# A hybrid encoder layer on one core: input projections in pairs by seven products, ahead of a recurrence whose preparation is split in two

## The chip, the cores and the metric

The kernel runs on one core of a Trainium2 chip. The metric is device time in microseconds (us) of one execution. Engines are named as the profile names them: PE (TensorE matmul), PEld (its weight loads), DVE (VectorE), ACT (ScalarE), POOL (GpSimd), SP (SyncE, which issues most DMAs).

## The reference, cut to what matters

Two batches of 512 tokens, width 1024, pass one layer with shared weights.

```python
h = _rmsnorm(x, norm_mix_g[l])
gates, p_a, pq, pkv, pkr = _split(h @ w_in[l], IN_SPLITS)      # 4416 columns
p_a = _token_shift(p_a, shift_mu[l])                           # previous and next token mixed in
y_a = _rwkv7_branch(p_a, ...) @ w_oa[l]
y_b = _mla_branch(pq, pkv, pkr, ...) @ w_ob[l]
g_a, g_b = jnp.split(jax.nn.sigmoid(gates), 2, axis=-1)
x = x + (g_a * y_a + g_b * y_b) @ w_out[l]
h = _rmsnorm(x, norm_ffn_g[l])
gt, up = jnp.split(h @ w_gu[l], 2, axis=-1)
x = x + (jax.nn.silu(gt) * up) @ w_down[l]
```

Branch A is a recurrence over the tokens, forwards and backwards, for 8 heads of 64; each step does

```python
sa = jnp.einsum('bhvk,bhk->bhv', state, kk_t)
state = (state * w_t[:, :, None, :] - sa[..., None] * (kk_t * a_t)[:, :, None, :]
         + v_t[..., None] * k_t[:, :, None, :])
return state, jnp.einsum('bhvk,bhk->bhv', state, r_t)
```

Here r, k and v are projections (`rkv`), w and a come from low-rank products (`w2`), kk is k scaled and normalised in each head, and the output is normalised per head, gets a bonus term and a low-rank gate (`g2`). Branch B is latent attention, 8 heads: queries, keys and values are products of small normalised latents; softmax over 512 keys.

## The kernel before, in words

**Precision.** Most products take operands split into a high and a low part (`split`: a copy on ACT, a subtraction on DVE). `mm3` issues three matmuls for each pair of operands, of 128 rows by 512 columns as a rule. Products of the recurrence, the transposes, and probabilities times values take plain 32-bit operands.

**Front.** Eight tiles of x are normalised and transposed (`norm_T`) into operands `h_hi`, `h_lo` of each batch. `proj` multiplies one tile of 128 columns of w_in with both batches, 8 inner blocks, 48 matmuls. There are 35 tiles: 4 low-rank inputs (w, a, g, x), 12 of r, k, v (`rkv_tiles`, three for each of four head pairs), 16 gates (`gate_tile`), 3 latents. First come the four low-rank tiles, then the low-rank up products (`lora_phase`), the first pair's r, k, v, and the latents. Results go to DRAM tensors (`rwkv_in`, `gate_d`, `mla_d`).

**Recurrence.** A unit is one batch and one pair of heads; there are eight, two batches for each pair in turn. Tokens are cut in 8 chunks of 64, both directions at once. `prep` loads r, k, v, makes the key norm and the bonus term, scans the decays, builds the scaled tiles `kra`, `krb`, `bt`, `kt`, multiplies them to `gx` and `gy`, and transposes (`tb`, `tk`, `vp`). `lanes` solves the triangular systems of all chunks on POOL (31 steps of a multiplication and an addition, tiles `lt`, `el`). `merge` joins the 32-wide halves (`zp`, `xp`). `state` walks the 8 chunks (`s`, `o`, copies `rs`, `sva`, `svb`), and `post` normalises the output.

**Order.** During the recurrence the order of PE is written out by `drive`. It keeps a planned clock, adds a planned cost for every matmul, and always lets the first thread in its list go on whose waiting time is over: state, post, merge, preparation, fill, combine. A thread yields planned microseconds (times 1.2 for state, 1.4 for the others), or a condition. The fill thread has the remaining r, k, v tiles, all gates and the attention; a step of it is one matmul. A unit's preparation goes in one thread, one unit after the other, and its second half waits for the state of two units before. The merge of a unit is planned 40 us after its solve is issued. Outside `drive` the framework orders the instructions.

**Attention** computes keys, values and queries as it needs them, then for each head and 128 queries: scores (`sc`), maximum, exponential, division by the sum, four transposes (`pt`), and for two heads together probabilities times values (`pav`).

**After it.** `combine` multiplies both branches' outputs with w_oa and w_ob (`pab`), scales by the gates and adds; `project` multiplies with w_out (`pwo`). Batch 0 combines and projects, then batch 1. Then come the norms and the feed-forward part, which already takes pairs of blocks by seven products: `gate_up` (`pgA`, `pgB`, `pgC`) and the down products (`dx`, `dy`, `dz`).

Of the kernel before, what the change touches and what calls it, by code (L numbers as in the profile page):

```python
# [47 lines left out]
PB = (5, 1)  # L48
# [22 lines left out]
OFFS = 200000, 150000, 120000, 100000, 0, 0  # L71
# [8 lines left out]
C0 = 18  # L80
PL = 3.5
# [13 lines left out]
ES = 'gg'  # L95
EF = 'gggg'
# [8 lines left out]
def trunk(ctx, tc, outs, x, w_in, w2, g2, w_uq, w_ukk, w_ukv, w_oab, w_out, w_gu, w_down,  # L105
# [42 lines left out]
    nc.sync.dma_start(idn, ident)  # L148
# [16 lines left out]
    rwkv_in = [[dram.tile([P, 8, S], F32, name=f"rwkv_in{b}{p}") for p in range(NPAIR)] for b in range(NB)]  # L165
# [58 lines left out]
    front = ctx.enter_context(ExitStack())  # L224
    psf = ppool(front, "psf")

    def pf(name):
        return psf.tile([P, S], F32, tag="f", bufs=NF, name=name)

    def mg(name):  # L230
        return psf.tile([P, S], F32, tag="mg", bufs=2, name=name)
# [5 lines left out]
    class _PS:  # L237
        def tile(self, shape, dt, tag=None, name=None):
            return psf.tile([P, S], F32, tag=PSTAG[0], bufs=PSTAG[1], name=name)

    class _PF:
        def tile(self, shape, dt, tag=None, name=None):
            return pf(name)

    e_d = [dram.tile([32, CH, CH], F32, name=f"e_d{i}") for i in range(2)]
    nt_d = [dram.tile([32, CH, CH], F32, name=f"nt_d{i}") for i in range(2)]
    bo_d = [[dram.tile([P, S], F32, name=f"bo_d{b}{p}") for p in range(NPAIR)] for b in range(NB)]
    mla_d = [dram.tile([P, 3, S], F32, name=f"mla_d{b}") for b in range(NB)]
    kr_d = [dram.tile([64, S], F32, name=f"kr_d{b}") for b in range(NB)]

# [4 lines left out]
    hst = ctx.enter_context(ExitStack())  # L255
    hp = pool(hst, "h", side="right")
    h_hi, h_lo = [None] * NB, [None] * NB
    for b in HORD:
        h_hi[b] = hp.tile([P, KD, S], F32R, name=f"h_hi{b}")
        h_lo[b] = hp.tile([P, KD, S], F32R, name=f"h_lo{b}")  # L260
    wp = pool(hst, "w1", side="right")
# [4 lines left out]
    def norm_T(t, xt, sp, newps, gcol, hi, lo, name):  # L266

        ss = sp.tile([P, 1], F32, tag="nss", bufs=4, name=f"nss_{name}{t}")
        ht = sp.tile([P, D], F32, tag="nh", bufs=NHB, name=f"nh_{name}{t}")
        nc.scalar.activation(ht, xt, AF.Square, accum_out=ss)  # L270
        rstd_cols(ss, ss, 1, 1.0 / D, RMS_EPS)
        nc.vector.tensor_scalar_mul(ht, xt, ss)
        ts = slice(t * P, (t + 1) * P)
        for g in range(2):
            ps = newps(f"nt_{name}{t}{g}")
            tr4(ps, lambda i: ht[:, (g * 4 + i) * P:(g * 4 + i + 1) * P])
            gs = slice(g * 4, (g + 1) * 4)
            sc = sp.tile([P, 4, P], F32, tag="nsc", bufs=NSB, name=f"nsc_{name}{t}{g}")
            nc.vector.tensor_mul(sc, ps.rearrange("p (k t) -> p k t", k=4),
                                 cc(gcol + g * 4, 4).unsqueeze(2).to_broadcast([P, 4, P]))  # L280
            nc.scalar.copy(hi[:, gs, ts], sc)
            vg(NLO[t * 2 + g]).tensor_sub(lo[:, gs, ts], sc, hi[:, gs, ts])

    def proj(ti, name):
        res = [pf(f"pj_{name}{b}") for b in range(NB)]
        wt = []
        for q in range(2):
            raw = wp.tile([P, 4 * P], F32, tag="wraw", bufs=2, name=f"wraw_{name}{q}")
            nc.sync.dma_start(raw, w_in[ti][:, q * 512:(q + 1) * 512])
            hi = wp.tile([P, 4 * P], F32R, tag="whi", bufs=2, name=f"whi_{name}{q}")  # L290
            lo = wp.tile([P, 4 * P], F32R, tag="wlo", bufs=2, name=f"wlo_{name}{q}")
            split(hi, lo, raw)
            wt.append((hi, lo))
# [1419 lines left out]
```

## Time and profile before

| | |
|---|---|
| median of 2 runs | 1835.03 us (1832.98 to 1837.08) |
| profiled execution | 1835.74 us, span 1834.0 us |
| PE busy | 1734.3 us, 95% of the span |
| DVE, ACT, POOL busy | 1116.9, 771.0, 642.2 us |
| DMA moved | 208.97 MB, 114 GB/s |
| granted PE clock, mean | 0.978 |

A page of the profile gives busy time of each engine, the chain of work that ended last, and groups of instructions with mean durations. A matmul's recorded duration holds its latency, which overlaps with the next one; what it takes of PE's time is seen in the chain, where a piece ends as the next begins. Plain 32-bit matmuls stand as two records each.

### The profile page before, as it was taken

The numbers are of one execution on the slowest core, as the hardware profiler recorded it, in microseconds if no ns is written. First come the engines' busy times: TensorE is split into PE (matmuls) and PEld (weight loads), VectorE is DVE, ScalarE is ACT, GpSimd is POOL, SyncE is SP. The second block draws the span as 40 slices with busy tenths as digits, with TensorE's granted clock in tenths as the row PEclk, the third lists the DMA queues.
The fourth block names the chain that finished last, engine by engine and source line by source line (L and its number), as shares of the span: only waits on it lengthen the run. The fifth ranks groups of instructions, "written<-read, shape, count | busy, mean of one in ns | idle before, by whom it ended". The sixth has DMA issues, their size and how long they took to land.

```text
span 1834.0 us, 31000 instructions
## 1 busy us (share of the span) xinstructions
PE 1734.3 (95%) x11676; PEld 1365.7 (74%) x11676; DVE 1116.9 (61%) x1957; ACT 771.0 (42%) x1496; POOL 642.2 (35%) x992
## 2 busy tenths in 40 slices
PE   6999999999999998899989999699999999989997
PEld 6887766777677775565657979578888888868886
DVE  6633555635364455877786556865655555588757
ACT  5434343333434334656663233333333333335445
POOL 3012345362635536161112123853434333100006
PEclk8999989999999998999999999899999999999999
DMA  4354433425343334212067551022222222274342
GB/s 163 123 175 163 123 107 82 124 71 136 81 125 106 89 113 119 61 36 55 21 233 249 190 178 35 24 81 93 103 95 84 92 81 92 98 273 134 121 139 92
DMA packets 185333, 208.97 MB, mean 114 GB/s; under 512 B 102816, under 2 KB 114464, under 8 KB 185184
## 3 DMA queue, kind: packets, MB, share of 16 engines
q1 hardware_dynamic: 184320, 205.48, 35.4%
q8 instruction: 92, 1.51, 0.3%
q10 hardware_dynamic: 720, 0.98, 0.2%
q0 software_dynamic: 144, 0.52, 0.1%
q14 instruction: 57, 0.47, 0.1%
HBM read 147.70 MB, written 59.24 MB: 113 GB/s over the span
## 4 chain that ended last, share of the span: by engine, by line
PE 70%; DVE 9%; DMA 8%; POOL 5%; issue 3%; ACT 2%; SPq 1%; DVEq 0%; POOLq 0%; ACTq 0%
PE pgC L125 9%; PE pj_gt L125 8%; PE pgB L125 6%; PE pgA L125 6%; PE pj_rkv L125 5%; PE dx L125 5%; PE dy L125 3%; PE s L125 3%; PE pab L125 2%; PE sc L125 2%; PE pav L125 2%; PE pj_mla L125 2%; DMA wor<-in_w_out 2%; PE o L125 2%; PE gx L125 2%
## 5 line engine op out<-in xcount | busy, mean ns | idle before, releaser
L839 POOL TENSOR_TENSOR lt<-lane,el 128x126 f32<-128x126 f32 (+22 forms) x248 | 93.4, 377 | 38.1 <-DMA lane<-nt_d 19.6
L841 POOL TENSOR_TENSOR el<-el,lt 128x126 f32<-128x126 f32 (+22 forms) x248 | 98.6, 398 | 19.0
L125 PE MATMUL pab<-yo,wab 128*128 128x512 f32 x384 | 94.7, 400 | 5.9 <-ACT yo L132 3.2
L125 PE MATMUL pj_gt<-h_hi,whi_gt 128*128 128x512 f32 x240 | 99.2, 413 | 0.0
L125 PE MATMUL pj_gt<-h_hi,wlo_gt 128*128 128x512 f32 x240 | 98.8, 412 | 0.1
L125 PE MATMUL pj_gt<-h_lo,whi_gt 128*128 128x512 f32 x240 | 98.1, 409 | 0.0
L125 PE MATMUL pwo<-woh,m 128*128 128x256 f32 x512 | 93.8, 283 | 0.1
L125 PEld LDWEIGHTS pab<-yo,wab 128*128 128x128 f32 x384 | 71.9, 191 | 26.0 <-DVE wab L133 4.2
L1203 POOL TENSOR_TENSOR s<-uraw 128x512 f32<-128x512 f32 x22 | 29.3, 1330 | 152.1 <-DMA uraw<-in_w_gu 152.1
L125 PEld LDWEIGHTS pwo<-woh,m 128*128 128x128 f32 x512 | 80.3, 192 | 0.6 <-ACT woh L132 0.3
L125 PE MATMUL pj_rkv<-h_hi,wlo_rkv 128*128 128x512 f32 x192 | 79.7, 418 | 0.0
L125 PE MATMUL pj_rkv<-h_lo,whi_rkv 128*128 128x512 f32 x192 | 79.1, 412 | 0.0
L125 PE MATMUL pj_rkv<-h_hi,whi_rkv 128*128 128x512 f32 x192 | 78.3, 408 | 0.0
L125 PE MATMUL pwo<-wol,m 128*128 128x256 f32 x256 | 72.4, 284 | 0.9 <-DVE wol L133 0.9
L1582 POOL TENSOR_TENSOR x<-x,dp 128x512 f32<-128x512 f32 x4 | 6.3, 1590 | 178.1 <-DVE x L1581 178.1
L1271 DVE TENSOR_TENSOR p<-p,pgC 128x512 f32<-128x512 f32 x22 | 15.1, 687 | 86.9 <-PE pgC L125 86.9
L919 ACT COPY sva<-s 64x128 f32<-64x128 f32 x64 | 16.5, 258 | 104.6 <-PE s L125 96.3
L1050 POOL TENSOR_TENSOR g<-g 128x512 f32<-128x512 f32 x16 | 24.9, 1554 | 92.7 <-DVE g L1048 84.5
L466 POOL TENSOR_SCALAR lut<-lut 128x512 f32<-128x512 f32 x32 | 20.5, 641 | 98.4 <-ACT lut L464 98.1
L125 PEld LDWEIGHTS pj_gt<-h_hi,wlo_gt 128*128 128x128 f32 x240 | 45.1, 188 | 9.5 <-DVE wlo_gt L133 0.8
L125 PEld LDWEIGHTS pj_gt<-h_hi,whi_gt 128*128 128x128 f32 x240 | 45.1, 188 | 8.6
L125 PEld LDWEIGHTS pj_gt<-h_lo,whi_gt 128*128 128x128 f32 x240 | 45.1, 188 | 8.4
(1559 smaller groups left out, 5552.9 us busy)
## 6 DMA issues: line engine op xcount, KB each, us to landing
graw<-in_w_gu SPq DMA_DIRECT2D x22, 512.0 KB, 3.5
uraw<-in_w_gu SPq DMA_DIRECT2D x22, 512.0 KB, 3.5
a_d<-a SPq DMA_DIRECT2D x21, 512.0 KB, 3.3
w<-in_w_down SPq DMA_DIRECT2D x42, 256.0 KB, 4.1
x<-in_x SPq DMA_DIRECT2D x16, 512.0 KB, 8.2
rwkv_in<-lut SPq DMA_DIRECT2D x32, 256.0 KB, 2.0
gate_d<-gtt SPq DMA_DIRECT2D x32, 256.0 KB, 2.5
wab<-in_w_oab SPq DMA_DIRECT2D x32, 256.0 KB, 3.6
```

The costliest lines, as they stand in the source:

```text
L125: pin(nc.tensor.matmul(out, lhsT, rhs, start=start, stop=stop, **kw), n if out.shape[0] > 64 else n / 2)
L466: nc.gpsimd.tensor_scalar(t, t, f, f, op0=ALU.mult, op1=ALU.add)
L839: eng.tensor_mul(lv, lane[:, s, s + 1:].unsqueeze(1).to_broadcast([P, m_, n]), el[:, 0:m_, s].unsqueeze(2).to_broadcast([P, m_, n]))
L841: eng.tensor_add(ev, ev, lv)
L919: nc.scalar.copy(sva[HA, :, c], s2[HA])
L1050: nc.gpsimd.tensor_add(g_[:, 0], g_[:, 0], g_[:, 1])
L1203: vg(ES[min(j, 1)]).tensor_add(s1, a21, a22)
L1271: nc.vector.tensor_add(p1, p1, x_)
L1582: nc.gpsimd.tensor_add(xs(1, t, 1), xs(1, t, 1), p5[t])
```

## The change

**Projections.** All projections come before the recurrence. Two tiles of 128 columns and the two batches form a two-by-two block product with the inner dimension halved; `pair` makes it from seven products of 12 matmuls (in place of eight) with sums of weight blocks on DVE and sums of results. The batch-side operands are `H11`, `H21`, `H22`, `U1` to `U4`, made at the start from the norms of x. The tile that is left over goes through `single`. `early` begins four gate pairs before all operands exist.

**Work beside the projections.** `Fill` puts steps of other work between the products: latent norms, keys and values, queries (multiplied with the rotary tables and the softmax scale), the low-rank up products, and the key norms and bonus terms of all units. Their results go to DRAM (`k_d`, `v_d`, `q_d`, and a ninth plane of `rwkv_in`). The low-rank up product takes 64-row halves of its weights for the two directions, instead of zero-padded 128 rows.

**Recurrence.** Units go batch by batch. `prep_a` loads, scans, makes `gx` and starts the solve; `prep_b` makes `krb`, `gy` and the transposes. They are two threads; `prep_a` may be three units ahead of the state, so `kra`, `arb`, `e_d`, `nt_d` get a third set. The copies `rs`, `z` and those from `xp` go to ACT.

**Fill of the recurrence.** Attention loads its keys, values and queries; the division by the sum comes after the product with the values, by a broadcast that four transposes make. Then come the attention branch's products of both batches, branch A's of batch 0, and the output projection of batch 0, whose result goes to DRAM. Branch A of batch 1 waits for the last unit; then come its output projection and the rest as before. The feed-forward part changes only in where its tiles lie and in how the output projection is cut (512 columns at a time).

```diff
+    def prod(ps, wt, op_, first):
+        for k in range(KH):
+            ks = slice(k * P, (k + 1) * P)
+            run(mm3(ps, wt[0][:, ks], wt[1][:, ks], op_[0][:, k], op_[1][:, k],
+                    start=(first and k == 0), stop=False, skip_group_check=True))
...
+    def pair(nm, ta, tb, use, p1=None):
...
+        s1, s2 = tmp(1), tmp(2)
+        vg(PES[0]).tensor_add(s1, a21, a22)
+        vg(PES[1]).tensor_sub(s2, s1, a11)
+        y = abank(1, f"pjB{nm}")
+        prod(y, w_block(s1, f"wS1{nm}"), U1, True)
+        p5 = wp.tile([P, S], F32, tag="p5", bufs=2, name=f"p5w{nm}")
+        nc.scalar.copy(p5, y)
+        yield
...
+            nc.vector.tensor_add(e1, x_, p1)
+            yield
+            prod(c, w_block(a12, f"wA12{nm}"), H21, False)
+            use(0, 0, c)
+            yield
+            s4 = tmp(4)
+            vg(PES[2]).tensor_sub(s4, a12, s2)
+            prod(y, w_block(s4, f"wS4{nm}"), H22, False)
+            nc.vector.tensor_add(e1, e1, y)
+            use(0, 1, e1)
...
+        prod(x_, w_block(s3, f"wS3{nm}"), U3, False)
+        nc.vector.tensor_add(p5, p5, x_)
+        use(1, 1, p5)
...
+        prod(x_, blk, U4, False)
+        nc.vector.tensor_add(p1, p1, x_)
+        use(1, 0, p1)
...
+    def products(gen, n):
+
+        for i in range(n):
+            next(gen, None)
+            fill.step()
+            if i == min(2, n - 1) and late:
+                run(late.pop())
+                fill.step()
+        late.append(gen)
...
+    fill.q.append(norm())
+    rkv_pair(0)
+    fill.drain()
+    sl.close()
+    fill.q.append(keys_values())
+    rkv_pair(1)
+    fill.drain()
+    fill.q.append(queries())
+    gate_pair(4)
+    rkv_pair(2)
+    fill.drain()
...
-        def prep(self, free):
+        def prep_a(self, free):
...
+        def prep_b(self, free):
...
-                nc.vector.tensor_copy(rs_, s1)
+                nc.scalar.copy(rs_, s1)
...
-    order = [(b, p) for p in range(NPAIR) for b in range(NB)]
+    order = [(b, p) for b in range(NB) for p in range(NPAIR)]
...
+    def prep_a_thread():
+        for i in range(NU):
+            if i > 1:
+                yield has("prep", i - 2)
+            yield from units[i].prep_a(has("state", i - 3) if i > 2 else 0)
+            done.add(("a", i))
+
+    def prep_b_thread():
+        for i in range(NU):
+            yield has("a", i)
+            yield from units[i].prep_b(has("state", i - 2) if i > 1 else 0)
             done.add(("prep", i))
...
+    def fill_thread():
+        with ExitStack() as sa:
+            yield from attention(pool(sa, "attn", side="right"))
+        with ExitStack() as s3:
+            ec = pool(s3, "ec", side="right")
+            yield from branch((0,), 1, ec, pf)
+        with ExitStack() as s3:
+            ec = pool(s3, "ec1", side="right")
+            yield from branch((1,), 1, ec, pf)
+        for i in range(NPAIR):
+            yield has("post", i)
+        yield has("prep", NU - 1)
+        rp0st.close()
+        mtiles(m0st, 0, side="right")
+        with ExitStack() as s3:
+            ec = pool(s3, "ec0", side="right")
+            yield from branch((0,), 0, ec, pf, mt[0])
...
+    def tail_thread():
         for i in range(NU):
             yield has("post", i)
```

More of the change, by code (lines that the diff above doesn't have):

```diff
@@ L80 @@
 C0 = 18
+FPRIO = 400
 PL = 3.5
@@ L95 @@
 ES = 'gg'
+PES = 'vvvvv'
 EF = 'gggg'
@@ L263, in vg, with operand @@
+    def operand(pl, name):
+        return [pl.tile([P, KH, S], F32R, name=f"{name}{i}") for i in range(2)]
     def vg(e):
         return nc.gpsimd if e == 'g' else nc.vector
[L266 to L282, printed above, removed]
@@ L548, in finish, with attention @@
+    def attention(ap):
+        pending, sums = [], {}
         def finish():
```

1091 lines of the change are left out of this document (642 added, 449 removed).

## The prediction

> **What bounds the kernel now.** I read the page's totals first, then the busy time by stage, then the chain of waits, because totals over a program with unlike stages say only which engine to look at.
>
> ```profile
> span 1834.0 us, 31000 instructions
> PE 1734.3 (95%) x11676; PEld 1365.7 (74%) x11676; DVE 1116.9 (61%) x1957; ACT 771.0 (42%) x1496; POOL 642.2 (35%) x992
> ```
>
> ```profile
> core 0: us, PE busy (x) PEld busy (x) DVE busy (x) ACT busy (x) POOL busy (x), PEclk, DMA share, GB/s
> 0.00:28.00 28.00, 12.09 (x57) 10.57 (x58) 19.85 (x36) 15.82 (x28) 11.76 (x18) 0.87 0.52 193
> 28.00:190.00 162.00, 159.75 (x762) 131.84 (x763) 77.33 (x126) 72.60 (x119) 33.06 (x47) 0.97 0.44 149
> 190.00:915.00 725.00, 690.14 (x6683) 502.62 (x6681) 420.42 (x922) 323.56 (x705) 322.06 (x731) 0.98 0.33 90
> 915.00:1107.00 192.00, 181.95 (x984) 146.40 (x985) 122.58 (x222) 77.97 (x147) 35.12 (x23) 0.98 0.61 203
> 1107.00:1186.00 79.00, 64.31 (x471) 59.53 (x469) 61.80 (x83) 32.34 (x58) 47.62 (x37) 0.95 0.09 28
> 1186.00:1834.00 648.00, 626.11 (x2724) 514.68 (x2724) 414.92 (x572) 248.73 (x441) 192.54 (x137) 0.98 0.33 112
> ```
>
> The stages are: start; first projections; recurrence with everything that fills it; the two branch products and the first output projection; the second output projection with the norms; the feed-forward part. PE is busy in nearly all of each but the first and fifth. So the time is mostly a sum of PE work, and I price that work from the chain of waits (columns: start, us, what), where a piece counts only the time until the next one starts.
>
> ```profile
> 41.84 10.91 PE pj_a L125 x48
> ...
> 404.06 0.38 PE s L125 x8
> 404.44 0.38 PE o L125 x8
> 404.82 1.59 PE pj_gt L125 x6
> 406.42 0.38 PE s L125 x8
> 406.80 0.23 PE o L125 x8
> 407.03 1.13 PE pj_gt L125 x4
> 410.51 3.62 PE pj_gt L125 x15
> ...
> 1254.74 2.72 PE pgC L125 x12
> ```
>
> A 512-column matmul costs 2.72/12 = 0.2267 us in an undisturbed run (10.91/48 is the same). Between pieces of the recurrence (s, o) a run of n such matmuls costs more: 1.59 − 6×0.2267 = 0.23, 1.13 − 4×0.2267 = 0.22, 3.62 − 15×0.2267 = 0.22. The excess belongs to the return from small tiles to large ones, not to the matmul. One unit's period of 80 us, all of PE and then the gate projections alone:
>
> ```profile
> 519.00:599.00 80.00, 79.39 (x819) 58.94 (x817) 40.11 (x84) 32.01 (x68) 40.13 (x93) 1.00 0.37 101
> 519.00:599.00 80.00, 50.12 (x181) 31.17 (x179) 4.76 (x8) 1.00 0.37 101
> ```
>
> The recurrence's own work on PE is 79.39 − 50.12 = 29.3 us of 80; the rest is fill, of which 50.12 − 181×0.2267 = 9.1 us is returns. So two things can bound this stage: the fill, or the order in which units are prepared. The second is what sets the period.
>
> ```profile
> L125 PE MATMUL gx<-kra,bt x256: 269/269/320, 197.6 to 783.3; 64*64 64x128 f32 x128
> L125 PE MATMUL s<-sva,kra x256: 219/222/370, 278.2 to 896.8; 128*64 128x64 f32 x128
> 439.00:489.00 50.00, 9.81 (x176) 1.00 0.30 77
> 521.00:568.00 47.00, 9.67 (x179) 1.00 0.33 87
> 678.00:735.00 57.00, 10.85 (x184) 0.91 0.40 106
> 458.00:495.00 37.00, 24.11 (x65) 1.00 0.25 68
> ```
>
> First and last gx are seven units and 586 us apart, about 80 us each. The next three rows are state phases (tile s alone): 47 to 50 us, 57 where PE ran dry between gates and attention. The last is one triangular solve on POOL: 37 us, 24 of them busy. Neither explains 80; one preparation thread does, which runs statistics, gx, gy and transposes of a unit before it begins the next.
>
> **The change, part by part: the front.** All 35 projection tiles go ahead of the recurrence. Seventeen pairs take seven products of 12 matmuls and the single tile 48, 17×84 + 48 = 1476 in place of 35×48 = 1680. The low-rank products keep 96 and drop from 48 to 32; queries, keys and values (144) come out of attention. That is 1748 × 0.2267 = 396 us. The start stays at 28. The stage 28–190 held 480 projection and 144 low-rank matmuls, 141.5 us; its other 20.5 us (latent statistics, the first unit's key norm, bubbles) stay. Seven more units' key norms move here, each by
>
> ```profile
> 414.99 0.79 PE ss_kk L125 x8
> 421.37 0.44 PE rbp_kk L129 x4
> 423.43 1.05 PE bp L125 x2
> ```
>
> 2.3 us, 16 in all. What covers this is the vector engine keeping up. Its prices (first row min/median/max ns, the others mean):
>
> ```profile
> L133 DVE TENSOR_TENSOR wlo_rkv<-wraw_rkv,whi_rkv x24: 670/693/876, 76.3 to 340.8; 128x512 fp32r<-128x512 f32 x24
> L310 DVE SCALAR_TENSOR_TENSOR shr<-pj_rkv,col,shr x24: 735/750/751, 89.0 to 360.0; 128x511 f32<-128x511 f32 x24
> L1262 DVE TENSOR_TENSOR e<-e,pgB 128x512 f32<-128x512 f32 x22 | 15.1, 687 | 26.9 <-PE pgB L125 26.9
> ```
>
> A pair has 7 weight splits (0.693), 4 weight sums and 5 result sums (0.687): 11.0 us against 84×0.2267 = 19.0 on PE; an r/k/v pair adds 8 shifts (0.75), 17.0 us. It fits, barely, and key-norm or query work joins both engines. The operand sets for the second batch cost about 11 vector operations per 128 tokens, 4×11×0.69 = 30 us, while only four pairs' first two products (4×2×2.72 = 22 us) are ready: 10 us of starvation, bounds 0 and 20. The front is 28 + 396 + 20.5 + 16 + 10 = 471 us. Small moves (stores on ACT's queue, the added key, query and value stores and reloads) I cost at nothing: DMA is 0.44 busy there.
>
> The low-rank matmuls now pair two 64-row halves; I leave them at full price because no large 64-row pair is in this trace. The Trainium skill (TensorEngine Tiling (Array Packing), Key Properties) says that different tiles of the array can run in parallel, which would halve 96 of them; that estimate is 11 us less, a sum of 1771, and no row here shows it for 512 columns.
>
> **The recurrence and its fill.** Own work: 29.3 − 2.3 = 27 us a unit, 216. Scores keep 192 matmuls, 43.5 us. Transposes and the product with values:
>
> ```profile
> L129 PE MATMUL pt<-idn,pr 128*128 128x128 f32 x256 | 40.4, 282 | 10.4 <-DVE pr L610 5.3 <-ACT pT L554 2.2 <-ACT pr L608 1.5
> L125 PE MATMUL pav<-pT,vt 128*64 128x512 f32 x128 | 39.7, 629 | 0.0
> ```
>
> 40.4 + 39.7, and 32 new transposes for the delayed division (32/256 × 40.4 = 5): attention 129. Four branch products (384) and the first batch's output projection (192) make 576×0.2267 = 131. Returns: 9.1 a unit, 73 if all stay, 768×9.1/181 = 38 if they go by matmul; I take the middle, 56. Waits that fill does not cover: the first loads, 8 (bounds 4 and 15); three pauses at a branch's start (18 planned us times slack 1.4 = 25, in which PE has 27/48 of its time used), 3×11 = 33 (0 to 75); the second unit's merge, planned by time alone while its solve stands behind the first's 37 us on POOL, with PE's written order behind it, 10 (0 to 25). Sum 216 + 129 + 131 + 56 + 51 = 583 us.
>
> The other bound is the units' own pace. From the first gx to the first s is 81 us, and ahead of gx stand a load and some 16 vector operations of 0.69:
>
> ```profile
> 255.43 5.05 DMA c<-rwkv_in
> ```
>
> 5 + 11, together 97. Then states may follow each other at 48 us: prep of a unit no longer waits for its predecessor's gy and transposes, and buffers are three deep. POOL has 40.1 a unit, less than 48. Then 12 for the last post (6.3 planned us of waits times 1.4, and its matmuls), and 52 for the last branch (pause 25, a load 5, 96 matmuls 22): 97 + 384 + 12 + 52 = 545, under 583. What is late next is therefore PE's sum.
>
> Two moves inside a state step:
>
> ```profile
> L895 DVE COPY rs<-s 128x128 f32<-128x128 f32 x8 | 2.3, 286 | 6.5 <-PE s L125 6.5
> L919 ACT COPY sva<-s 64x128 f32<-64x128 f32 x8 | 2.1, 258 | 17.1 <-PE s L125 15.7 <-POOL lt L839 1.3
> ```
>
> The rs copy goes from DVE to ACT at about the same duration; behind it on ACT wait exponentials, ahead of it may stand one. Zero while fill covers it; if not, between −2 us (64 times 0.028) and +17 us (64 times one such ACT copy in front of it). The added waits (a preparation for the state three units back, a merge for the state two back) are conditions of the written order: behind them stand only later units.
>
> **The sum.** The second output projection with its norms (79) and the feed-forward part (648) keep their work. 471 + 583 + 727 = 1781 us of span, and 1.74 more around it (the profiled run took 1835.74 with a span of 1834.0, 0.7 above the median of the runs, 1835.03). Forecast 1782, 2.9% less.
>
> **Rivals.**
> - *All returns stay* (73): 583 + 17, total 1800. The 0.22 us that does not depend on the run's length speaks for it; against it, a period of 48 instead of 80 leaves fewer pieces of fill between steps. Beside it: the Trainium skill (TensorEngine Tiling (Array Packing), Key Properties) says that a change of tiling mode drains TensorE, so the price would go with the recurrence's steps; by that rule the sum is 1800. The 0.22 us agrees with it. Chance 0.12.
> - *The vector engine bounds the front.* If r/k/v pairs with key norms or queries take 4 us longer each, 6×4 = 24, and the start 10 more: 1816. For it: 17.0 of 19.0 us; against it: 77.33 of 162 in the same stage now. Chance 0.12.
> - *Slower: the period does not fall.* With pace p the whole is 471 + 97 + 8p + 64 + 727 + 1.7 = 1361 + 8p: at 80 us 2001, even with the kernel before at 59, over 2% slower from 64. The mechanism would be POOL and the SP queue: three units' solves, decay products and DMAs in one order, so that merge waits although preparation ran ahead. For it: 37 us of solve for 24 busy, and fill that is gone from the recurrence can't hide it. Against it: 40.1 us of POOL in a period. Chance 0.13.
> - *All waits covered* (43 of the 51 gone and no starvation): 1729. Chance 0.10.
> - *It does not do what it says*: 204 matmuls come back as extra passes, 46 us, 1828. The counts above speak against it. Chance 0.03.
>
> **Numbers.** The forecast has 0.50; its own range is 1740 to 1805. About 2% (1798 and 1872) is what a measurement of this kernel can tell from no change. Faster: 0.45 of the forecast, 0.10 of the covered waits, 0.05 of the returns: 0.60. Slower: 0.13. Same: the rest, 0.27. The range 1715 to 1850 takes in all but the slow rival and the far end of the covered waits.
>
> **What would show it.** The last projection ends near 470 us; then eight state phases follow at 46 to 50 us with no gap of 30 between them; the last branch ends near 1054; the feed-forward stages still take 727. Wrong would be: gaps between states with PE idle and merge or solve as releaser (slow rival); DVE above 90% in the r/k/v pairs with PE waiting on weight splits (vector rival); runs of large matmuls between states near 0.23 us each (returns gone).

## The result

The changed kernel takes 2096.59 us (median of two runs, 2095.24 to 2097.94) against 1835.03: a ratio of 1.1425 with a 95% interval of 1.1362 to 1.1489, so 14% slower where 1782 was forecast. The profiled run took 2097.94 us with a span of 2096.2, against 1781 us of span in the sum of the prediction: 315 us more.

The page's totals, and the busy time by stage (columns: from:to and length, then busy us and instructions of each engine, the granted PE clock, the DMA share, GB/s):

```profile
span 2096.2 us, 30228 instructions
PE 1768.3 (84%) x11056; PEld 1354.4 (65%) x11056; DVE 1207.2 (58%) x1914; ACT 871.9 (42%) x1718; POOL 653.7 (31%) x966
```

```profile
25.00:82.00 57.00, 38.67 (x150) 29.50 (x149) 50.57 (x73) 23.59 (x44) 26.39 (x14) 0.79 0.23 74
82.00:452.00 370.00, 363.63 (x1614) 292.92 (x1614) 235.67 (x391) 160.07 (x276) 7.13 (x11) 0.99 0.41 135
452.00:582.00 130.00, 64.17 (x190) 40.30 (x188) 48.83 (x84) 46.63 (x75) 15.04 (x18) 0.59 0.50 171
582.00:689.00 107.00, 79.91 (x697) 53.60 (x697) 79.95 (x126) 70.48 (x157) 68.35 (x128) 0.89 0.50 128
689.00:1191.00 502.00, 393.63 (x4938) 279.97 (x4937) 241.46 (x480) 237.16 (x583) 263.26 (x591) 0.86 0.37 96
1191.00:1293.00 102.00, 71.47 (x274) 53.18 (x275) 45.84 (x64) 26.83 (x45) 28.44 (x19) 0.79 0.58 207
1293.00:1436.00 143.00, 105.30 (x437) 81.25 (x435) 77.04 (x100) 43.78 (x76) 48.01 (x38) 0.86 0.26 84
1436.00:2096.00 660.00, 640.84 (x2724) 515.59 (x2724) 414.86 (x572) 248.04 (x441) 191.40 (x137) 0.98 0.33 110
```

Before, PE was busy 95% of the span and nearly all of most stages. Now it is 84%, and three stages have holes. The projections are dense and end at 452 us. Then PE is busy for 64 of 130 us, at a granted clock of 0.59, before attention and the recurrence begin at 582. From the first state (689) to the last one's end (1191) PE is busy 394 of 502 us. From there to the feed-forward part, 177 of 245. Set beside the prediction's steps:

| part | forecast, us | measured, us | difference |
|---|---|---|---|
| front, up to attention | 471 | 582 | +111 |
| from there to the first state | 97 | 107 | +10 |
| first state to the end of the last | 384 | 502 | +118 |
| from there to the feed-forward part | 181 | 245 | +64 |
| feed-forward part | 648 | 660 | +12 |

The 181 is what the prediction leaves: 1781 − 648 − (471 + 97 + 384). The sum of the last column is 315.

**The front's end.** The chain of waits between 452 and 582 us (start, us, what), in three pieces:

```profile
473.88 4.12 DMA kx<-rwkv_in
478.02 0.73 ACT kk L763
...
479.46 1.88 PE ss_kk L127 x8
481.62 1.65 POOL rn L769
483.29 0.62 ACT rb_kk L190
483.96 1.12 PE rbp_kk L131 x4
485.08 1.72 PE bp L127 x2
486.82 0.70 DVE kx L778
...
542.69 1.72 PE bp L127 x2
544.43 0.70 DVE kx L778
545.15 1.96 DMA bo_d<-kx
...
567.43 2.09 PE lug L127 x4
569.54 0.60 ACT lugt L646
570.16 8.92 DMA rwkv_in<-lugt
```

One key norm goes through a DMA, ACT, PE, POOL, ACT, PE and DVE, one behind the other. PE has 4.7 us of it (1.88 + 1.12 + 1.72) at a granted clock of 0.57 from 473 to 545 us; before, beside projections and at full clock, the same three pieces took 2.3. Eight norms fill 479 to 545, and from 488 to 506 the chain runs through the first unit's loads and scans, which stand among them in DVE's written order. The norms begin only when the low-rank up products (332 to 472) have ended, and the low-rank gate's follow them. In the code each of these steps opens its memory when the one before has closed its own, and on SP its loads stand behind the other's stores; the trace doesn't tell the two apart. The up products themselves stop for a while: from 405 to 448 us PE is busy all 43 us, with projections, and one up product begun at 404.5 is ended at 449. So their lateness is not only the length of a chain; PE's written order, which the framework makes here, put the projections ahead of them.

**A state.** Here the same view for a state window and the gap after it in the kernel before, and then a state in the middle and the last one of the changed kernel:

```profile
439.00:489.00 50.00, 47.01 (x522) 34.23 (x520) 19.90 (x49) 16.60 (x41) 30.78 (x73) 1.00 0.30 77
489.00:521.00 32.00, 31.87 (x289) 24.06 (x290) 18.93 (x33) 14.07 (x24) 8.67 (x20) 1.00 0.51 142
```

```profile
833.00:889.00 56.00, 46.92 (x671) 33.55 (x670) 35.00 (x68) 35.19 (x89) 30.80 (x63) 0.99 0.34 70
889.00:896.00 7.00, 6.40 (x43) 2.65 (x42) 2.81 (x5) 4.12 (x7) 6.11 (x15) 1.00 0.36 112
1151.00:1191.00 40.00, 30.09 (x349) 22.41 (x347) 17.83 (x38) 10.04 (x26) 12.99 (x17) 0.72 0.54 179
```

Before, DVE did 19.90 us of work in the 50 us of a state and 18.93 in the 32 us between two states, where the next unit's merge, scans and decays lay. Now the gap is 7 us and DVE and ACT do 35 us each in the window of a state. The states follow each other as intended, but with all of the neighbours' work beside them they last 68, 61, 56, 62, 71, 53, 51 and 39 us (first to last of each unit's 184 records of s matmuls), 461 in all against 396 before. The last one, beside which no unit is prepared, takes 39.

### The profile page after: what moved, and what is told of

It is laid out like the page before. It is cut to its first block, busy times and chain, and to the rows that moved or that the text cites. A ratio compares the mean times of both kernels' runs of the same rounds, so it can differ in the third digit from the quotient of the medians.

```text
span 2096.2 us, 30228 instructions
## 1 busy us (share of the span) xinstructions
PE 1768.3 (84%) x11056; PEld 1354.4 (65%) x11056; DVE 1207.2 (58%) x1914; ACT 871.9 (42%) x1718; POOL 653.7 (31%) x966
## 4 chain that ended last, share of the span: by engine, by line
PE 59%; POOL 11%; DMA 10%; DVE 9%; ACT 4%; issue 4%; SPq 2%; ACTq 0%; DVEq 0%; POOLq 0%
PE pgC L127 8%; PE pgB L127 6%; PE pgA L127 5%; PE dx L127 4%; POOL el L1159 3%; POOL lt L1157 3%; PE pjCg L127 3%; PE dy L127 3%; PE pwo L127 2%; PE pjCr L127 2%; PE pjBg L127 2%; PE pjAg L127 2%; PE pab L127 2%; PE pjAr L127 2%; PE pjBr L127 2%
## 5 line engine op out<-in xcount | busy, mean ns | idle before, releaser
L127 PE MATMUL pwo<-woh,m 128*128 128x512 f32 x256 | 90.2, 428 | 31.9 <-ACT woh L134 31.8
L127 PEld LDWEIGHTS pwo<-woh,m 128*128 128x128 f32 x256 | 52.5, 206 | 48.0 <-ACT woh L134 37.8
L127 PE MATMUL s<-sva,bka 128*64 128x64 f32 x224 | 27.7, 253 | 52.8 <-DVE svb L1238 52.6
L127 PE MATMUL sc<-kt,qh 128*128 128x512 f32 x128 | 51.7, 470 | 8.1 <-ACT qh L134 3.2
L127 PE MATMUL pwo<-wol,m 128*128 128x512 f32 x128 | 55.4, 434 | 1.4 <-DVE wol L135 1.4
L127 PE MATMUL pav<-pT,vt 128*64 128x512 f32 x128 | 52.1, 711 | 4.0 <-ACT pT L883 4.0
L927 DVE TENSOR_REDUCE mx<-sc 128x1 f32<-128x512 f32 x64 | 43.7, 685 | 17.8 <-PE sc L127 16.6
L929 ACT ACTIVATE pr<-sc,mx 128x512 f32<-128x512 f32 x64 | 44.1, 689 | 22.2 <-DVE mx L927 20.3
L1534 POOL TENSOR_TENSOR s<-graw,uraw 128x512 f32<-128x512 f32 x22 | 29.2, 1329 | 62.1 <-DVE S_2l L135 4.0
L131 PE MATMUL pt<-idn,pr 128*128 128x128 f32 x256 | 41.5, 287 | 5.9 <-ACT pr L929 5.9
```

What stands on the lines that cost most here:

```text
L127: pin(nc.tensor.matmul(out, lhsT, rhs, start=start, stop=stop, **kw), n if out.shape[0] > 64 else n / 2)
L131: pin(nc.tensor.transpose(ps[:, t * P:(t + 1) * P], src(t), idn), P / 1200)
L927: nc.vector.tensor_reduce(mx, sc, axis=AX.X, op=ALU.min)
L929: nc.scalar.activation(pr, sc, AF.Exp, scale=-1.0, bias=mx, accum_out=sm[:, qb * 2 + e:qb * 2 + e + 1])
L1534: vg(ES[min(j, 1)]).tensor_sub(s3, a11, a21)
```

## The experiments

Each was run once beside the kernel before, which took 1829.4 to 1834.7 us in these runs. The changed kernel's own two runs differ by 2.7 us; I don't read differences under about 8.

### The front: is its end work or a chain?

**Half of the side work.** Queries, key norms and low-rank up products for batch 0 only; whatever batch 1 needs is read from batch 0's.

```diff
-                for b in range(NB):
+                for b in range(1):
...
-        nc.sync.dma_start(qf, q_d[b][hd])
+        nc.sync.dma_start(qf, q_d[0][hd])
...
-                nc.sync.dma_start(c_, rwkv_in[b][p][:, 4 + d])
+                nc.sync.dma_start(c_, rwkv_in[0][p][:, 4 + d])
```

> Beside the projections, queries, key norms, bonus terms and both low-rank up products are made for batch 0 alone, and batch 1 loads batch 0's; the rest is unchanged. Theory 1 (this side work is a chain of its own, one memory block after the other, that ends 130 us after the last projection): half of about 295 us of the chain goes, the front ends with the projections near 460 us in place of 582, and the whole falls by 110 to 130 us to about 1975. Rival 2 (the front is the sum of PE work): 112 matmuls at 0.227 and four key norms at 2.3 go, 34 us, to about 2062.

2013.88 us, 83 less. Attention's first score comes at 493 us in place of 585, while the projections end at 437, only 15 earlier; the states sum to 472, so nothing came from them. That is less than theory 1's 110 to 130 and more than twice the rival's 34. The front ends with the side work, not with the projections; whether it is late by its own chain or by its place in PE's written order, this run doesn't separate.

**The same work, less of it in a row.** First the key norms of two batches side by side, then also a fourth staging buffer for the low-rank up products.

```diff
+                held = []
                 for b in range(NB):
...
-                    r_, k_, v_ = (x3[:, i] for i in range(3))
+                    held.append((b, nm, [x3[:, i] for i in range(3)]))
+                mid = []
+                for b, nm, (r_, k_, v_) in held:
...
+                for (b, nm, (r_, k_, v_)), (kk, rn) in zip(held, mid):
```

> The key norms of the two batches of one pair of heads are written side by side (both loads, both statistics, then both broadcasts) in place of one after the other; the work is the same. Theory 1, the front's end is a chain of latencies: the eight norms take 8 us each now (479 to 543 us); four pairs of about 9 would give back 25 to 30 us, attention begins at about 555 in place of 582 and the time is about 2070. Rival 2, the front's end is a matter of how much work there is: no change beyond 8 us.

2091.20 us. The eight norms take 478 to 531 us in place of 479 to 544 (first to last of their matmuls), and the first score comes 13 us earlier (572): latency, then, but half of what theory 1 gave, and of the 13 only 5 reach the end, a difference too small to read.

```diff
-            return wp.tile([P, 512], F32, tag="s", bufs=4, name=f"ws{i}{nm}")
+            return wp.tile([P, 512], F32, tag="s", bufs=3, name=f"ws{i}{nm}")
...
-                            t = lp.tile([P, S], F32, tag="lut", bufs=3, name=f"lut{b}{p}{e}{d}")
+                            t = lp.tile([P, S], F32, tag="lut", bufs=4, name=f"lut{b}{p}{e}{d}")
...
-                    t = lp.tile([P, S], F32, tag="lut", bufs=3, name=f"lugt{b}{p}")
+                    t = lp.tile([P, S], F32, tag="lut", bufs=4, name=f"lugt{b}{p}")
```

> The front alone: key norms side by side as in the run before (2091.2 us), and the low-rank up products get four staging buffers in place of three (the weight sums give one up, three in place of four). Theory 1, each step of the chain waits for a store to give its buffer back: attention begins 10 to 25 us earlier than with the key norms alone, time about 2072. Rival 2, the staging buffers do not pace it: within 8 us of 2091.

2075.51 us, near theory 1's number, but the first score moves only 5 us further (567). The other 11 us came behind it (the last state ends at 1169 in place of 1182, 13 of the 16 us), which theory 1 does not say. So staging is a small part of this chain.

### The states: what makes 60 out of 40?

I took the suspects one by one, since each one stands in the list of waits.

**The copies moved to ACT.** rs and half of the merge's copies go back to DVE.

```diff
-                nc.scalar.copy(rs_, s1)
+                nc.vector.tensor_copy(rs_, s1)
...
-                    nc.scalar.copy(z_[Q[2 * h + 1]], zp[Q[2 * h + 1], 0:NCH])
+                    (nc.scalar.copy, nc.vector.tensor_copy)[h](z_[Q[2 * h + 1]], zp[Q[2 * h + 1], 0:NCH])
```

> The state's copy rs and the merge's copies z and xp go back from ACT to DVE; all else is the changed kernel. Theory 1 (each state step waits in ACT's queue behind the attention's exponentials and copies): the eight states fall from 461 us in sum toward the 394 of the kernel before, the first five most, the whole by 50 to 70 us to about 2035. Rival 2 (states are slow because more units' preparation stands between their steps): states within 15 us in sum, the whole between 2080 and 2105.

2101.76 us, states' sum 465: the copies' place is not it.

**The decay product on DVE** in place of POOL.

```diff
-                    nc.gpsimd.tensor_mul(sp_[HA], sva[HA, :, c], pcb[HA])
+                    nc.vector.tensor_mul(sp_[HA], sva[HA, :, c], pcb[HA])
```

> The decay product of the state (sp, two a chunk, 56 chunks) goes from POOL to DVE, so that no step of a state has to go through POOL's written order, where the triangular solve stands. Theory A, POOL's order paces the states: of the changed kernel's waits between 689 and 1200 us, 28.1 us are DVE waiting for sp and 25.2 us ACT's; these go, the states after the first sum to about 430 in place of 461 us, the time falls to about 2060 (2045 to 2075). Rival B, each hop of a state queues on every engine and the next one takes over what one gives up: states' sum within 15 of 461, time within 10 of 2097. Rival C, DVE becomes the line that is waited in: slower, by 56 x 2 x 0.2 = 22 us at most.

2100.82 us, sum 467. Rival B's numbers.

**The pauses at a branch's start** taken out, and **the first half of a preparation held back** until the unit before is prepared.

```diff
-C0 = 18
+C0 = 2
```

> The planned pause at the start of each branch product goes from 18 to 2. Theory 1 (the first batch's output projection runs after the recurrence because its branch products start too late by the plan): it moves under the last states, and the whole falls by 40 to 60 us to about 2045. Rival 2 (what holds it is the condition that all units are prepared): branch A of batch 0 still starts near 1190, and the whole falls by under 20 us.

```diff
-            if i > 1:
-                yield has("prep", i - 2)
+            if i > 0:
+                yield has("prep", i - 1)
```

> The first part of a unit's preparation waits until the second part of the unit before is done, as in the kernel before. Theory 1 (units prepared further ahead crowd the state's steps and make them longer): states fall below 54 us on average from 58, with gaps between them. Rival 2 (the crowd does not matter, the queue of ACT does): states stay at 58, gaps open, and the whole gets longer by 20 us or more.

2088.95 and 2080.32 us. Without the pauses branch A of batch 0 begins at 1146 in place of 1192, but the last four states go from 71, 53, 51, 39 to 54, 61, 56, 58, and the last ends at 1226: most of the gain is given back. With the preparation held back the states are even (57, 60, 60, 59, 60, 58, 45, 56), gaps of 26, 13 and 20 us open between some of them, and the last ends at 1221; still the whole is 16 us faster, so running further ahead, a part of the change, bought nothing. Neither of the two expectations fits: the states don't fall below 54 on average, and the time doesn't grow.

**The fill.** Attention left out, and then, with all work done, the whole fill put behind the last state.

```diff
-        with ExitStack() as sa:
-            yield from attention(pool(sa, "attn", side="right"))
...
-        nc.sync.dma_start(t, (y_d, o_d)[e][b][p])
+        nc.sync.dma_start(t, (y_d, k_d)[e][b][p])
```

> Attention is left out (the branch products read the keys in its place, so the output is another one): 129 us of TensorE work by the prediction, with its copies on ACT and reductions on DVE. Theory B, the states are long because their hops queue behind the operations of the fill: states stand at 48 to 50 us from the first on, their sum falls from 461 to about 395, the time to about 2030. Rival D, the stage is bound by TensorE's sum: the time falls by the whole 129, to about 1968. Rival E, the pace is the unit's own chain (preparation, merge, state) whatever runs beside it: states stay at 53 to 65 us and the time within 25 of 2097.

```diff
     def fill_thread():
+        yield has("state", NU - 1)
```

> Attention, branches and output projection begin only when the last state is written, so the eight states run with nothing beside them but their own preparation, solves, merges and posts. Only the states' pace is to be read, the time must be longer (fill alone is some 129 + 131 us of TensorE work, and more where it waits). Theory B, hops queue behind the fill: pace 45 to 49 us (the last chunks of the changed kernel, with almost nothing beside them, take 5.2 us each, 8 x 5.2 = 42, and 3 to 7 between states). Rival E, the unit's own chain: pace 56 to 63 as in the changed kernel, with the states' idle time put down to merge, solve or preparation.

2050.00 and 2300.50 us. Without attention the states still sum to 456, and the time falls by 46, a third of the 129 that attention was to cost PE. With no fill at all they sum to 449. The views by stage of that run, two states in the middle and the last:

```profile
806.00:867.00 61.00, 43.20 (x599) 33.84 (x598) 25.80 (x54) 22.37 (x58) 37.20 (x89) 0.64 0.31 71
871.00:937.00 66.00, 42.45 (x599) 33.62 (x598) 25.88 (x54) 21.84 (x57) 35.63 (x84) 0.63 0.28 64
1124.00:1159.00 35.00, 27.75 (x318) 21.55 (x318) 7.65 (x24) 5.69 (x18) 6.36 (x13) 0.50 0.02 9
```

PE has nothing to do but the units' own work, and a state beside the others still takes 60 and 66 us, against 35 alone. In the last one a chunk takes 4.1 us, the bare chain of its hops, and that at the lowest clock of the three. Theory B falls: not the fill, but something of the units themselves.

**Standing in line.** One chunk of the changed kernel, in order of time (start, us, engine, line, what; in brackets the engine's idle time before it and what ended it):

```profile
905.08 0.40 PE L127 MATMUL s<-rs,e 64*64 64x64 f32 x8
...
907.00 0.53 POOL L1143 MEMSET el<- 128x512 f32 x1 [5.51 <-DMA e_d<-el]
907.48 1.05 POOL L1116 TENSOR_TENSOR kt<-kt,pc 128x512 f32<-128x512 f32 x1
...
908.83 0.40 POOL L1231 TENSOR_TENSOR sp<-sva,pc 64x128 f32<-64x128 f32 x1
909.26 0.26 ACT L1237 COPY sva<-s 64x128 f32<-64x128 f32 x1 [5.95 <-POOL sp L1231]
...
910.55 0.45 DVE L1182 STREAM_TRANSPOSE tp<-e 128x256 f32<-128x256 f32 x1 [5.86 <-DMA e<-e_d]
910.92 0.39 DVE L1071 TENSOR_TENSOR nt<-gx,msk 128x256 f32<-128x256 f32 x1
911.23 0.41 DVE L1072 TENSOR_TENSOR arb<-gx,msk 128x256 f32<-128x256 f32 x1
...
911.67 0.29 DVE L1238 COPY svb<-s 64x128 f32<-64x128 f32 x1
...
912.02 0.27 PE L127 MATMUL s<-sva,bka 128*64 128x64 f32 x1 [4.82 <-DVE svb L1238]
```

The product s is ready at 905.5 and its two copies run at 909.3 and 911.7. ACT waits for sp, which stands on POOL behind the next solve's clear, which waits for the last solve's store. DVE waits at the merge's transpose for a load, with two mask products behind it, and only then copies svb. Three engines stand in their written order on work of other units. That this is what makes the states long is a theory; the next runs test its pieces.

**The merge written later**, after the fifth chunk of the state before; then with a second buffer for the solve's result; then with the merge's loads ahead of its transposes; then that with sp on DVE.

```diff
+            if i:
+                yield has("chunk", units[i - 1].nm, 4)
             yield from units[i].merge()
```

> A unit's merge is written only after the fifth of the eight chunks of the unit before it (in the changed kernel it is written by planned time, in that state's first half). Nothing else changes. Theory F, the states are long because DVE, in its written order, stands at the merge's first transpose until the next unit's solve has landed (948.3 to 957.2 us in the run with the fill put last), with the running state's copies behind it, and POOL and ACT after DVE: chunks of 12 to 26 us go, the states sum to 380 to 420 in place of 461 us, the time falls to 2030 (2010 to 2060). Rival G, solves follow each other at 63 to 71 us by their own chain (preparation, store, load, 36 us of steps) and the states wait for them wherever the merge is written: sum within 15 of 461 or gaps between states in its place, time within 15 of 2097.

```diff
-                el = rp.tile([P, m1 - m0, 32], F32, tag=f"el{m0}", bufs=1, name=f"el{nm}{m0}")
+                el = rp.tile([P, m1 - m0, 32], F32, tag=f"el{m0}", bufs=2, name=f"el{nm}{m0}")
```

> As the run with the late merge, and the solve's result has two buffers (z shares tp's to make room), so that POOL does not stand until the store of one solve has landed before it clears the next (906.75 us in the changed kernel, some 5 us after the solve's last step). Theory F: 2 to 5 us a unit less than with the late merge alone, time 2000 to 2045. Rival G: within 8 us of the run with the late merge.

```diff
                 got.append((e_, ntl))
+            yield late
+            for i, (e_, ntl) in enumerate(got):
```

> As the run with the late merge (2079.6 us, states' sum 447 us), but the merge's loads are issued when the solve is due and only its transposes and products come after the fifth chunk, so that DVE does not stand at the first transpose for a load issued just ahead of it (30.1 us in 7 waits there). Theory F: the states' sum falls by about 25 to 420, time about 2052 (2040 to 2068). Rival (another line takes over): within 10 of 2079.

> The split late merge and the decay product sp on DVE, two lines relieved at once. Theory I, several lines hold the state at once and each takes over from the other: the two together gain more than the sum of the two alone (split alone, and +4 for sp alone), by 15 us or more. Rival: the sum of the two alone, within 8.

| kernel | time, us | states' sum, us |
|---|---|---|
| changed | 2096.59 | 461 |
| merge late | 2079.61 | 448 |
| and a second buffer | 2080.35 | 453 |
| merge late, loads ahead | 2075.07 | 442 |
| and sp on DVE | 2067.03 | 442 |

In the first of these the merge's transposes still wait for their load (engine, line, what ended the wait: us in total, times, longest):

```profile
DVE tp L1182 <- DMA e<-e_d: 30.1, 7, 8.7
```

With the loads ahead it is 22.2 us in 7 waits, so that edit did little of what it was for. The second buffer does nothing, though the wait that it removes stands in the chunk above. The split with sp on DVE is 8 us faster than the split alone, where sp alone lost 4: 12 better than the sum of the two, between theory I's 15 and its rival's 8, and the states' sum doesn't move. Each line is worth 17 us or less, and none alone is the cause.

**The solve cut short**, and **the post left out**.

```diff
-            for s in range(31):
+            for s in range(8):
```

> The triangular solve takes 8 of its 31 steps (the output is another one), so POOL has some 30 us a unit less. Theory H, POOL's written order paces the units (36 us of solve, and some 27 of decay products, clears, loads and waits for the states in the same line): states' sum from 461 to 360 to 400, time about 2020. Rival F, the states are slow by what stands ahead of them on DVE, ACT and TensorE: sum above 435, time within 30 of 2097, the first state some 30 us earlier because its own solve is shorter.

```diff
+            nc.sync.dma_start(y_d[b][p], os_)
             yield YO1
+            return
```

> The group norm after each state is left out (the raw state output is stored). Theory P, the post's chain, DVE to POOL's power to ACT's copy (ACT waits 11.9 us for POOL there, 40.0 in the run with the fill last), holds up the next state: states' sum 461 to about 430, time 2097 to about 2065. Rival: within 10 us of 2097 but for about 8 us at the end, where the last post is on the path.

2058.35 us with a sum of 425, and 2089.12 with a sum of 460. Without 23 of the 31 steps on POOL (all 31 take 34 to 41 us a unit in the changed kernel), the second to the fifth state still last 63, 57, 57 and 61. The numbers lie between theory H's and its rival's: the solve is worth 36 of the 461 us, 20 of them in the first state, which goes from 68 to 48; the post is worth nothing.

**All preparation of later units left out.** Units 2 to 7 walk their chunks on what units 0 and 1 left; attention, branches and posts stay beside them.

```diff
         for i in range(NU):
             if i > 1:
-                yield has("prep", i - 2)
+                done.add(("a", i))
+                continue
```

> Units 2 to 7 are not prepared: no loads, products, transposes, solve or merge of their own; their states run on what units 0 and 1 left (the output is another one). Attention, branches and posts stay. Theory J, a state is slow by the preparation and merge of later units that stand beside it (in the kernel before these lay half in the 31 us between states): states 2 to 7 at 38 to 46 us as the last one now (40), pace under 50, last state ends near 1075, time about 1985 (1960 to 2010). Rival, the fill beside it: states stay at 52 or more, time above 2040.

1926.24 us. The states last 57, 46, 41, 44, 39, 44, 46 and 58 us (the last beside branch A and the output projection of batch 0), 373 in all; the pace from state to state is 49 us, and the last ends at 1078. Two of them:

```profile
789.00:830.00 41.00, 38.16 (x421) 24.79 (x422) 15.20 (x37) 19.75 (x52) 7.20 (x15) 1.00 0.08 27
881.00:919.00 38.00, 27.68 (x338) 20.92 (x339) 14.55 (x34) 9.91 (x25) 7.53 (x15) 0.73 0.35 111
```

This is theory J, and the time is even below its 1960 to 2010. The first of these states has attention beside it and PE busy for 38 of 41 us: a state bears fill well. What it does not bear is the preparation of other units: 113 us of the last state's end, and 57 more behind it, because the fill, too, gets ahead when the preparations are gone (branch A of batch 0 begins at 1002 in place of 1192). How those 88 us of the states' sum (461 − 373) split between loads, products, transposes, solve and merge is known only for the solve (36) and the merge (13 to 19, by its place); the rest was not taken apart.

### What adds up

> Late merge, two buffers for the solve's result, key norms side by side, four staging buffers, and no pause at a branch's start, together. Where the causes are separate (front, states, tail) the gains add: about 60 + 6 + 15 + 8, time about 2005 (1985 to 2030). Where they are one chain that the front or the states alone set, no better than the best of them by more than 8 us.

> The repairs that gained alone, together: split late merge with sp on DVE (2067.0, 30 under the changed kernel), key norms side by side with four staging buffers (2075.5, 21 under it). If front and recurrence are one after the other, 2097 - 30 - 21 = 2046; if one hides the other, not below 2060.

Late merge, second buffer, side-by-side norms, four staging buffers and no pauses: 2052.00 us, 45 less, where these gain 17, 21 and 8 alone (the 2005 expected had booked the late merge at 60). The split merge, sp on DVE and the two repairs of the front: 2048.29, 48 less where 51 was the sum. Front and recurrence lie one behind the other, and their gains add. Of the versions that leave nothing out it is the fastest, and it is still 12% above the kernel before. By this account the missing 213 us would need the side work and the preparations to have the projections beside them again, which this order of the work excludes; no run tried it.

## Why the prediction was wrong

**Right.** The count and price of the front's matmuls: the trace has the 1748 that were counted, and in the dense stage 1614 in 370 us is 0.229 each, and the last projection ends at 452 where the text said "near 470". Starvation at the start: PE is busy 38.67 of 57 us in the second stage, 18 us idle, inside the bounds of 0 and 20 though not the 10 taken. DVE does not bound the projections (235.67 of 370 us), so that rival was rightly low; only in the start is DVE nearly full, 50.57 of 57 us. The first preparation, 97 against 107; the second unit's merge, 10 taken with bounds 0 to 25, and PE waited 17.3 us for it. States follow each other without gaps of 30 us: 4 to 9 us lie between them, and with the first half of the preparation held back again gaps of 26, 13 and 20 us return, so the preparation's order did have its part in them.

**The first step that failed: the front as a sum of PE work** ("Seven more units' key norms move here", at 2.3 us, "16 in all", and queries, keys and values as 144 matmuls). I priced the side work by its matmuls, and named DVE as what hides it: 471 us in the sum, 582 in the run. That cover lasts only while there are projections. The side steps come one after the other, and 130 us of them come after the last projection; with half of them left out the front ends 92 us earlier. Even their price on PE was too low there: 4.7 us a key norm in place of 2.3, at a granted clock of 0.57. In the trace of before, the same steps lay beside projections or the recurrence and cost nothing visible; I asked what they cost PE, not how long they take from first to last. Why they come so late is shown in part only: the norms' latency (side by side they gain 13 us), and the written order of PE, which let the projections pass.

**The second: 48 us a state.** The three windows quoted for it were true, but a state of before had half a unit's other work beside it and 32 us of gap for the rest. The preparation's order had its part in the gap, as the text said, but it doesn't follow that a state stays at 48 without it: 80 was state and gap together. When the gap went, its work went into the states: 66 us from state to state, and 49 in the run that leaves the later units' preparation out. What I held to be the bound, PE's sum of 583, was not one: from 582 to 1293 us PE is busy 545 of 711. (The 586 us over seven units are 84 a unit, not "about 80"; nothing hangs on it.)

**The third: what is late next at the end.** 181 us were to follow the last state; it took 245. Branch A of batch 0 has 96 matmuls left, its gate loads and the loads of w_out stand in one chain, and PE is idle from 1219.2 to 1242.2 us between the branch and the output projection:

```profile
1215.61 9.37 DMA g<-gate_d
...
1228.96 7.45 DMA g<-gate_d
...
1243.86 4.21 DMA wor<-in_w_out
1248.09 0.63 ACT woh L134
1248.74 0.70 DVE wol L135
1249.46 2.54 DMA wor<-in_w_out
```

I let these hide under fill that was itself behind. The last branch ends at 1293, 102 us after the last state, just as the sum had it (1054 − 952). But 131 of the 192 matmuls of batch 0's output projection are still to come then, and the whole difference falls into the term that was carried over from before: the second output projection with its norms, 79 in the sum, 143 in the run (PE busy 105.3 in place of 64.3, idle 38 in place of 15). The pauses, booked at 33, were worth 8; the rest of the end was not taken apart by a run.

**The rivals.** The slow one had the right side and the right condition, a pace that does not fall to 48: 66 us from state to state gives 1361 + 8 × 66 = 1889. Its mechanism, POOL and the SP queue, is a part as far as it was tried (the solve, 36 of the states' 461 us; sp on POOL, nothing; SP's queue was not tried). The rest of the way to 2098 is the front (111), the first state (10), the end (245 where its 1361 holds 64 + 79 = 143, so 102) and the feed-forward part (12), less 26 because the eighth state takes 39 and not 66. Its chance of 0.13 was too low: the row that should have raised it is the gap's, with 18.93 us of DVE work in 32. The price of a return from small to large tiles stays: between pieces of the recurrence, runs of four and six branch matmuls take 1.13 and 1.59 us (at 1132.83 and 1143.36 us), as in the prediction's rows. What the returns add to the time could not be told, since PE bounded nothing there.

## What to carry to other kernels

Work that hides under other work has two prices: what it takes of the busy engine, and how long its own chain is from end to end. When the cover moves, use the second.

A window in which a stage ran fast tells only what it costs beside what lay in that window. Before taking it as the pace, read the gap next to it and put the gap's work back in.

Where each engine keeps a written order, a latency-bound walk can be slowed by whatever waits ahead of it on any of three or four engines. Here freeing one of them showed little; leaving the companions out altogether showed what they cost.

## What the hardware showed that was not expected

**The granted clock stays at half without long gaps.** In the last state of the run with the fill put last, the clock was 0.50 over 35 us while PE's records cover 27.75 of them. From 1131 to 1159 us the longest gap between two of its matmuls was 1.5 us. A matmul of s takes there

```profile
L127 PE MATMUL s<-rs,e x56: 311/311/366, 1132.6 to 1159.0; 64*64 64x64 f32 x56
```

against a median of 218 ns for the same tile before. The Trainium skill (TensorE: Matmul & The Clock Gate, Part 1: The HAM clock gate) puts the half clock behind an idle window of about 3.4 us; here the clock stayed down through steady short work with no such gap, so an idle window of that length is not what kept it there. That it goes by how busy PE is would fit (from 1131 to 1159 us PE's records cover 21.56 of 28), but no run varied it. In time it did not matter: a chunk took 4.1 us at that clock, where the chunks of before, most of them at full clock, took 5.4 to 11.6.

**Two 64-row matmuls of 512 columns run at once.** The low-rank up products of the changed kernel, in order of time:

```profile
332.45 0.96 PE L127 MATMUL lu<-lw,w 64*128 64x512 f32 x6
```

Six of them from the first start to the last end take 0.96 us; one after the other, six of 0.2267 would be 1.36. The records of a pair start 3 to 6 ns apart. The rule that the prediction set aside for lack of a row (the Trainium skill, TensorEngine Tiling (Array Packing), Key Properties: different tiles work in parallel) holds here; its estimate of 11 us was right to make, but PE's time did not set the end of the front, so it can't be read in the whole.

**A slower matmul in the same stage.** In the feed-forward part twelve matmuls take 2.80 us for two of the three tiles where they took 2.72, at the same granted clock of 1.00 (1500 to 1530 us of both kernels). Before, then after:

```profile
1504.98 2.72 PE pgA L125 x12
...
1518.58 2.72 PE pgB L125 x12
```

```profile
1502.38 2.80 PE pgB L127 x12
1505.18 2.75 PE pgC L127 x12
1507.92 2.80 PE pgA L127 x12
```

Over the stage's 2724 matmuls that makes up about the 12 us of the last row of the table, 2% of the stage. The front's projections in the same run keep 0.2267 where nothing disturbs them. Where the operands lie in memory changed between the kernels; whether that is the cause was not tried.
